# First layer of a two-layer decoder step: projections in the order gates, queries, keys, values, cached keys paced with them, convolution norm on the token axis

## The chip, the cores and the metric

The kernel runs on one core of a Trainium2 chip. The metric is the device time of one execution in microseconds; less is better. TensorE multiplies (PE in the rows, PEld is its weight load), VectorE (DVE), ScalarE (ACT) and GpSimd (POOL) do elementwise work, and SyncE (SP, SPq in the rows) issues nearly all DMAs, strictly in the order in which the program writes them. The order of the other engines' instructions is set when the program is built, and each engine then runs its own list in order.

## What is computed

Two layers, each a mixer and a squared-ReLU MLP, with norms around them, for a prompt of 1024 tokens and 8 samples of 4 tokens (1056 columns together). The change is in the mixer of the first layer:

```python
proj = xn @ w_in                       # 1024 -> 2560: q 512, k 512, v 512, a 512, g 512
s = einsum(q, k) * scale               # 4 heads, two key maps each, causal
w = softmax(map 0) - lam * softmax(map 1)
attn = rms_norm(w @ v, subln_g) * (1 - lam_init)
u = a * sigmoid(g)
c = causal_depthwise_conv(u, 31 taps) + conv_b
c = silu(layer_norm(c over its 512 channels) * ln_g + ln_b)
mixed = concat(attn, c) @ w_out
```

The samples attend to 2048 cached keys and values each, read page by page (128 tokens) through a page table, and to their own new keys and values. New keys and values of all tokens are outputs, too.

## The kernel before

Activations lie as [channel, token] in 48 slabs of [128, 1056] fp32; a tile waits until a slab is free. Products of fp32 accuracy are three matmuls of 352 columns: each operand is split into a high and a low part, and TensorE adds hi*hi, hi*lo and lo*hi (`mm3`, L195 to L197). A weight unit is a load (`wraw`), a cast on ScalarE (L188) and a subtraction on VectorE (L189).

`mixer0` (L1488) does the 20 units of the input projection one after another in the order of `seq`: `12` to `15` are a, `16` to `19` are g, `0` to `3` are q, `4` to `7` are k, `8` to `11` are v. Each unit is three blocks of 24 matmuls, one for each chunk of 352 columns (`part`), and `whole` does what follows a finished unit.

Beside this foreground run background generators. After each block the foreground calls `pump(us)`, and each generator advances by that time multiplied by its rate, which is how instructions of several strands are interleaved as they are written:

- `convs` (rate CV): 31 taps for each of four channel blocks, one `scalar_tensor_tensor` of 1024 columns each on VectorE (L977). It adds up the four blocks on GpSimd (`cn`, L996), stores each block to `cd`, waits until all projections are written (`projected`) and starts `conv_norm`, which loads the four blocks again and normalises over channels.
- `decode_k` (rate RKI during the projections, RK after): loads pairs of key pages (`load`, three pairs ahead), turns them on TensorE (`turn`, L1142, evacuated on ScalarE or, after the projections, half on VectorE at L1147), and multiplies them with the samples' queries (`strips`, L1154); then the new keys and the softmax (`dec_softmax`) for each of two groups of samples.
- `decode_v` (rate RV): 64 pairs of value pages, multiplied with the weights (L1217).
- `tokens` turns the keys and the values into token rows for the outputs; the values are also stored to `vd`, from which each head loads them in the layout that its product needs.

After the projections comes `prompt` (L1431): for four heads and eight blocks of 128 queries each, `scores` (L1324 to L1372: two score products `sp`, maximum, exponential, difference), one block later `turn` (L1386, tile `wT`), and then `values` (L1401, tile `av`). At the block number TH it starts `conv_half`, which waits for `normed` and does the convolution's half of the output projection (24 blocks of 12 matmuls, tile `y`, L1099). `finish` (L1718) turns the attention's results (`aT`, L1729) after `head_norm` (GpSimd, L1420 to L1428) of the last head; then come weight preparations, the norm of the samples' result (`subln`, whose column sum is at L1029), and the attention half of the output projection with the post norm (`posts`).

Of the kernel before, what the change touches and what calls it, by code (L numbers as in the profile page):

```python
# [16 lines left out]
P = 128  # L17
# [822 lines left out]
LEADK, LEADV, RKI, RK, RV, SMW = 3, 6, 0.45, 1.4, 1.1, 6.0  # L840
# [4 lines left out]
TH, RC, RE = 24, 1.0, 1.0  # L845
KA, SL = 1, 1.0
CV, CN, DL = 0.7, 1.0, 5.0


class Step0(Step):  # L850
# [3 lines left out]
    def consts0(self):  # L854
# [67 lines left out]
        nc.vector.tensor_scalar(self.cv[:, 5:9], self.cv[:, 5:9], -1.0, None, op0=ALU.mult)  # L922
# [58 lines left out]
    def convs(self, tiles, cd):  # L981
# [3 lines left out]
        for k in range(4):  # L985
# [51 lines left out]
    def conv_norm(self, s, cd):  # L1037

        nc = self.nc
        acc = [self.S("acc") for _ in range(4)]  # L1040
        for k in range(4):
            self.dma(acc[k], cd[k])
        yield DL
# [12 lines left out]
        yield 4.0  # L1056
        yield from self.rows_rsqrt(s, T, 512, r)
        for k in range(4):
            nc.vector.tensor_mul(acc[k], acc[k], r)
            yield 2.0  # L1060
# [4 lines left out]
        self.normed = True  # L1065

# [59 lines left out]
    def decode_k(self, qs, ks):  # L1126
# [28 lines left out]

        for i in range(LEADK):
            load(i)
# [4 lines left out]
        for i in range(64):  # L1162
# [19 lines left out]
            if pr == 7:  # L1182
                while not self.kready:
                    yield 1.0
                sc = self.PS("sc")
                strips(sc, g, slice(0, NS), lambda s, h: ks[:, 32 * h:32 * h + 32])
                nc.vector.tensor_add(SB[:, NP:T], sc[:, :NS], self.nmask[g])
                yield 0.5
                self.bg_add(self.dec_softmax(g, SA, SB), 1.0)

    def decode_v(self, vs, aS):
# [3 lines left out]
        while not self.ready:  # L1195
# [85 lines left out]
    def head_load(self, h, qd, kd, vd):  # L1281

        q, v = self.S("q"), self.S("v")
# [5 lines left out]
        vv = v[:, :1024].rearrange("p (i d) -> p i d", i=8)  # L1289
# [1096 lines left out]
```

## Time and profile before

| | us |
|---|---|
| median of 3 runs (2711.63 to 2716.34) | 2712.2 |
| the profiled execution | 2710.83 |
| its span | 2709.1 |
| TensorE busy | 2524.2 (93%) |
| VectorE busy | 1709.3 (63%) |
| ScalarE busy | 1016.9 (38%) |
| GpSimd busy | 738.3 (27%) |

The shares are means over stages with different limits; the table by stage in the rows below tells more. A busy TensorE is not one at its peak: a matmul's end is modelled, and consecutive matmuls overlap, so the time that one takes of the queue is read from the starts of the next. The granted clock is a mean over the stretch, and it has two levels, 1.2 and 2.4 GHz: 1.00 is the upper all through, 0.50 the lower.

### The profile page before, as it was taken

The numbers are of one execution on the slowest core, as the hardware profiler recorded it, in microseconds if no ns is written. First come the engines' busy times: TensorE is split into PE (matmuls) and PEld (weight loads), VectorE is DVE, ScalarE is ACT, GpSimd is POOL, SyncE is SP. The second block draws the span as 40 slices with busy tenths as digits, with TensorE's granted clock in tenths as the row PEclk, the third lists the DMA queues.
The fourth block names the chain that finished last, engine by engine and source line by source line (L and its number), as shares of the span: only waits on it lengthen the run. The fifth ranks groups of instructions, "written<-read, shape, count | busy, mean of one in ns | idle before, by whom it ended". The sixth has DMA issues, their size and how long they took to land. (4 is left out here: it accounts for less than half of the span.)

```text
span 2709.1 us, 42679 instructions
## 1 busy us (share of the span) xinstructions
PE 2524.2 (93%) x16315; PEld 2392.4 (88%) x16315; DVE 1709.3 (63%) x3036; ACT 1016.9 (38%) x2034; POOL 738.3 (27%) x1090
## 2 busy tenths in 40 slices
PE   8999979789899999999999787799879999999998
PEld 7999855559799999999999776699779999999997
DVE  6777666763868554655545999951686767455435
ACT  6133345754441222222213466642552333412103
POOL 0110001112616875343402588710510000000004
PEclk9999989999999999999999899899889999999999
DMA  5353689663032223222222433213032233433221
GB/s 187 93 170 112 202 269 318 188 222 106 14 113 63 91 82 96 61 79 82 90 78 67 168 111 111 67 35 125 22 128 95 96 116 132 174 95 110 87 80 65
DMA packets 240868, 311.41 MB, mean 115 GB/s; under 512 B 27604, under 2 KB 168162, under 8 KB 240655
## 3 DMA queue, kind: packets, MB, share of 16 engines
q1 hardware_dynamic: 240331, 308.44, 35.3%
q8 instruction: 129, 2.11, 0.3%
q14 instruction: 76, 0.62, 0.1%
q10 hardware_dynamic: 332, 0.23, 0.0%
HBM read 235.33 MB, written 73.72 MB: 114 GB/s over the span
## 5 line engine op out<-in xcount | busy, mean ns | idle before, releaser
L195 PE MATMUL mm<-hh,whi 128*128 128x352 f32 x1536 | 498.2, 326 | 0.0
L197 PE MATMUL mm<-hh,wlo 128*128 128x352 f32 x1536 | 496.6, 323 | 0.0
L196 PE MATMUL mm<-hl,whi 128*128 128x352 f32 x1536 | 496.3, 323 | 0.0
L195 PE MATMUL mm<-zh,whi 128*128 128x352 f32 x1344 | 447.3, 334 | 0.2 <-ACT zh L218 0.2
L196 PE MATMUL mm<-zl,whi 128*128 128x352 f32 x1344 | 439.8, 327 | 3.2 <-DVE zl L219 3.2
L197 PE MATMUL mm<-zh,wlo 128*128 128x352 f32 x1344 | 437.3, 326 | 0.0
L293 POOL TENSOR_TENSOR ssq<-ssq,sq 128x352 f32<-128x352 f32 x72 | 72.8, 1011 | 935.6 <-ACT sq L292 934.8
L189 DVE TENSOR_TENSOR wlo<-wraw,whi 128x1024 fp32r<-128x1024 f32 x152 | 194.7, 1284 | 168.7 <-ACT whi L188 158.6
L196 PEld LDWEIGHTS mm<-hl,whi 128*128 128x128 f32 x1536 | 289.4, 188 | 0.5 <-issue 0.2
L195 PEld LDWEIGHTS mm<-hh,whi 128*128 128x128 f32 x1536 | 289.1, 188 | 0.6 <-issue 0.2
L197 PEld LDWEIGHTS mm<-hh,wlo 128*128 128x128 f32 x1536 | 289.1, 188 | 0.0
L188 ACT CAST whi<-wraw 128x1024 fp32r<-128x1024 f32 x152 | 158.6, 1047 | 284.2 <-DMA wraw<-in_w_ffn_down 153.8
L196 PEld LDWEIGHTS mm<-zl,whi 128*128 128x128 f32 x1344 | 257.0, 191 | 7.2 <-DVE zl L219 4.0
L195 PEld LDWEIGHTS mm<-zh,whi 128*128 128x128 f32 x1344 | 256.8, 191 | 5.8 <-issue 3.0
L197 PEld LDWEIGHTS mm<-zh,wlo 128*128 128x128 f32 x1344 | 256.8, 191 | 0.1
L597 DVE TENSOR_TENSOR y<-y,mm 128x352 f32<-128x352 f32 x312 | 155.1, 517 | 76.8 <-PE mm L197 74.9
L563 ACT ACTIVATE t<-t 128x352 f32<-128x352 f32 x96 | 47.7, 498 | 318.5 <-DVE t L562 318.5
L195 PE MATMUL mm<-xh,whi 128*128 128x352 f32 x480 | 160.5, 336 | 4.2 <-DVE xr L281 4.2
L774 DVE TENSOR_TENSOR y<-y,mm 128x352 f32<-128x352 f32 x144 | 74.9, 521 | 136.5 <-PE mm L197 136.5
L977 DVE SCALAR_TENSOR_TENSOR acc<-proj,keep,acc 128x1024 f32<-128x1024 f32 x120 | 156.3, 1303 | 3.0
L196 PE MATMUL mm<-xl,whi 128*128 128x352 f32 x480 | 157.1, 328 | 0.0
L197 PE MATMUL mm<-xh,wlo 128*128 128x352 f32 x480 | 157.1, 328 | 0.0
(533 smaller groups left out, 5532.9 us busy)
## 6 DMA issues: line engine op xcount, KB each, us to landing
pg<-in_cache_k SPq DMA_DIRECT2D x128, 256.0 KB
pg<-in_cache_v SPq DMA_DIRECT2D x128, 256.0 KB
wraw<-in_w_ffn_down SPq DMA_DIRECT2D x64, 512.0 KB
wraw<-in_w_ffn_up SPq DMA_DIRECT2D x36, 512.0 KB
hr<-hid SPq DMA_DIRECT2D x32, 528.0 KB
wq<-in_w_ffn_up SPq DMA_DIRECT2D x28, 512.0 KB
hres<-res SPq DMA_DIRECT2D x24, 528.0 KB
res<-y SPq DMA_DIRECT2D x24, 528.0 KB
```

Source lines behind the costliest of these rows:

```text
L188: nc.scalar.copy(hi[:, :n], raw[:, :n])
L189: (eng or nc.vector).tensor_sub(lo[:, :n], raw[:, :n], hi[:, :n])
L195: nc.tensor.matmul(out, wh, xh, start=first, stop=False)
L196: nc.tensor.matmul(out, wh, xl, start=False, stop=False)
L197: nc.tensor.matmul(out, wl, xh, start=False, stop=last)
L293: (nc.vector if k in YV else nc.gpsimd).tensor_add(s, s, q)
L563: nc.scalar.activation(t1, t1, AF.Square)
L597: nc.vector.tensor_add(yc, yc, pt)
L774: nc.vector.tensor_add(yc, yc, pt)
L977: nc.vector.scalar_tensor_tensor(acc[:, :NP], u[:, i:i + NP], w[:, k, i:i + 1], acc[:, :NP], op0=ALU.mult, op1=ALU.add)
```

## The change

Values and keys change places in `seq`, so that the keys are known four units before the projections end. Key pages are paced at 0.85 in place of 0.45, taps at 0.85 in place of 0.7, and `conv_half` may start at block 14 in place of 24. `decode_k` no longer waits for the new keys in its line: a finished group is kept in `held`, and `fresh` adds the new keys when they are there. The last block of the convolution stays on chip, and `conv_norm` is another one: it subtracts the mean straight from PSUM, sums the squares by matmuls of one column, so that the sums lie on the token axis (one number for each token, ten columns), takes the root there on VectorE with whole numbers and three Newton steps (`root`), and brings it back with a diagonal matmul for each block. The head's values are loaded apart from its q and k (`values_load`), in the second block of each head, and the first head's load of q and k follows the first key unit. `decode_v` waits for `projected` and for the samples' values.

```diff
-LEADK, LEADV, RKI, RK, RV, SMW = 3, 6, 0.45, 1.4, 1.1, 6.0
+LEADK, LEADV, RKI, RK, RV, SMW = 3, 6, 0.85, 1.4, 1.1, 6.0
-TH, RC, RE = 24, 1.0, 1.0
+TH, RC, RE = 14, 1.0, 1.0
-CV, CN, DL = 0.7, 1.0, 5.0
+CV, CN, DL = 0.85, 1.0, 5.0
...
-            self.dma(cd[k], a)
-            a = None
+            if k < 3:
+                self.dma(cd[k], a)
+                a = None
         while not self.projected:
             yield 1.0
-        self.bg_add(self.conv_norm(s, cd), CN)
+        gen = self.conv_norm(s, a, cd)
+        next(gen)
+        self.bg_add(gen, CN)
...
-        q, r = self.S("cq"), self.S("cr")
         for c in range(NCH):
             pt = self.PS("cs")
             nc.tensor.matmul(pt[:, :CH], self.ones.bitcast(F32), s[:, chunk(c)], start=True, stop=True)
-            nc.scalar.activation(r[:, chunk(c)], pt[:, :CH], AF.Copy, scale=1.0 / 512)
-            yield 0.6
+            for k in range(4):
+                a = acc[k][:, chunk(c)]
+                nc.vector.scalar_tensor_tensor(a, pt[:, :CH], -1.0 / 512, a, op0=ALU.mult, op1=ALU.add)
+                yield 0.6
+        rows = [b for c in range(NCH) for b in blocks(c)]
...
         for k in range(4):
-            nc.vector.tensor_sub(acc[k], acc[k], r)
-            nc.scalar.activation(s if k == 0 else q, acc[k], AF.Square)
-            if k:
-                nc.vector.tensor_add(s, s, q)
-            yield 2.5
-        yield 4.0
-        yield from self.rows_rsqrt(s, T, 512, r)
-        for k in range(4):
-            nc.vector.tensor_mul(acc[k], acc[k], r)
-            yield 2.0
+            sq.append(self.S("cq"))
+            nc.scalar.activation(sq[k], acc[k], AF.Square)
+            yield 1.1
+        for i, (t, n) in enumerate(rows):
+            for k in range(4):
+                nc.tensor.matmul(pt[:n, i:i + 1], sq[k][:, t:t + n], self.ones.bitcast(F32)[:, 0:1], start=k == 0, stop=k == 3)
...
+        self.root(x, y, t_)
+        yield 3.0
+        for c in range(NCH):
+            rb = self.PS("rb")
+            for t, n in blocks(c):
+                i = rows.index((t, n))
+                dg = self.H("t")[:, :P]
+                nc.vector.tensor_scalar(dg[:n, :n], self.ident[:n, :n], y[:n, i:i + 1], None, op0=ALU.mult)
+                nc.tensor.matmul(rb[:, t - c * CH:t - c * CH + n], self.ones.bitcast(F32)[:n, :], dg[:n, :n], start=True, stop=True)
+            yield 1.0
+            for k in range(4):
+                a = acc[k][:, chunk(c)]
+                nc.vector.tensor_mul(a, a, rb[:, :CH])
+                yield 0.6
...
+    def root(self, x, y, t):
+        nc = self.nc
+        nc.vector.tensor_copy(t, x.bitcast(I32))
+        nc.vector.tensor_scalar(t, t, -0.5, 1597463007.0, op0=ALU.mult, op1=ALU.add)
+        nc.vector.tensor_copy(y.bitcast(I32), t)
+        for _ in range(3):
+            nc.vector.tensor_mul(t, y, y)
+            nc.vector.tensor_mul(t, t, x)
+            nc.vector.tensor_scalar(t, t, -0.5, 1.5, op0=ALU.mult, op1=ALU.add)
+            nc.vector.tensor_mul(y, y, t)
...
+        held = []
+        def fresh():
+            while held and self.kready:
+                g, SA, SB = held.pop(0)
+                sc = self.PS("sc")
+                strips(sc, g, slice(0, NS), lambda s, h: ks[:, 32 * h:32 * h + 32])
+                nc.vector.tensor_add(SB[:, NP:T], sc[:, :NS], self.nmask[g])
+                self.bg_add(self.dec_softmax(g, SA, SB), 1.0)
...
-        while not self.ready:
+        while not (self.ready and self.projected and self.vready):
             yield 1.0
...
+    def values_load(self, h, vd):
+        v = self.S("v")[:, :1024].rearrange("p (i d) -> p i d", i=8)
+        self.dma(v, vd[:NP, h * P:(h + 1) * P].rearrange("(i p) d -> p i d", p=P))
+        return v
...
-                    raw[h + 1] = self.head_load(h + 1, qd, kd, vd)
+                    raw[h + 1] = self.head_load(h + 1, qd, kd)
+                if i == 1:
+                    for _ in self.vgen:
+                        pass
+                    V[h] = self.values_load(h, vd)
...
-        seq = [16, 12, 17, 13, 0, 1, 2, 3, 18, 14, 19, 15, 8, 9, 10, 11, 4, 5, 6, 7]
+        seq = [16, 12, 17, 13, 0, 1, 2, 3, 18, 14, 19, 15, 4, 5, 6, 7, 8, 9, 10, 11]
...
-                    if h == 1:
-                        first.append(self.head_load(0, qd, kd, vd))
+                    if h == 0:
+                        first.append(self.head_load(0, qd, kd))
...
-                    self.bg_add(self.tokens(list(kv), T, put_v), 0.2)
+                    self.vgen = self.tokens(list(kv), T, put_v)
+                    self.bg_add(self.vgen, 1.0)
```

Three places show how the instructions move. The first is TensorE between two blocks of the projections, four units before their end: key turns `kT` (four to a row) between the last matmul of one block and what follows. Before:

```order
L197 MATMUL mm_2891<-xh_106,wlo_2518 128x352
L1142 MATMUL kT_2919<-ident,pg_2671 128x128 x4
L1142 MATMUL kT_2934<-ident,pg_2791 128x128 x4
L1142 MATMUL kT_2940<-ident,pg_2791 128x128 x4
L1482 MATMUL tok_2946<-ident,proj_2013 128x128
```

And in the changed kernel, between two blocks of its last unit:

```order
L197 MATMUL mm_3959<-xh_106,wlo_3243 128x352
L1183 MATMUL kT_3996<-ident,pg_3871 128x128 x4
L1183 MATMUL kT_4002<-ident,pg_3871 128x128 x4
L1183 MATMUL kT_4017<-ident,pg_3892 128x128 x4
L1183 MATMUL kT_4023<-ident,pg_3892 128x128 x4
L1183 MATMUL kT_4038<-ident,pg_3987 128x128 x4
L195 MATMUL mm_4045<-xh_92,whi_3579 128x352
```

The turns between blocks become more: counted over the whole list, 264 stand ahead of the first score product before, all 512 in the changed kernel.

The second is SyncE where the first head's values are read back (`v<-vd`). Before, key pages follow:

```order
L96 DMA kd<-proj_2890 128x1056
L96 DMA q_3087<-qd 128x1024
L96 DMA k_3089<-kd 64x1024 x2
L96 DMA k_3090<-kd 64x1024 x2
L96 DMA v_3088<-vd 128x8x128
L1107 TENSOR_LOAD ptab
L96 ISA
L96 DMA pg_3127<-in_cache_k 128x512
```

In the changed kernel it stands directly behind the values' token stores, ahead of the convolution's blocks and the first value pages:

```order
L96 DMA out_new_v_prompt<-tok_4321 128x512
L96 DMA vd<-tok_4321 128x512
L96 DMA out_new_v_sample<-tok_4330 32x512
L96 DMA v_4334<-vd 128x8x128
L96 DMA acc_4352<-cd 128x1056
L96 DMA acc_4353<-cd 128x1056
L96 DMA acc_4354<-cd 128x1056
L1148 TENSOR_LOAD ptab
L96 ISA
L96 DMA pg_4374<-in_cache_v 128x512
```

What the first value product needs is now written, stored and read back within the attention's first blocks.

The third is ScalarE between the last cast of the attention's result (`zh<-aT`) and the square `sq` for the samples' column sum, behind which the output product stands on TensorE. Before (from the last two weight casts on):

```order
L188 CAST whi_6955<-wraw_6952 128x1024
L188 CAST whi_6961<-wraw_6958 128x1024
L1099 COPY y_6978<-mm_6979 128x352
L1099 COPY y_6978<-mm_6993 128x352
L1099 COPY y_6978<-mm_7007 128x352
L1099 COPY y_7021<-mm_7022 128x352
L1099 COPY y_7021<-mm_7036 128x352
L1099 COPY y_7021<-mm_7050 128x352
L1099 COPY y_7064<-mm_7065 128x352
L1099 COPY y_7064<-mm_7079 128x352
L1099 COPY y_7064<-mm_7093 128x352
L1099 COPY y_7107<-mm_7108 128x352
```

In the changed kernel:

```order
L1792 ACTIVATE zh_7182<-aT_7184,gain_h 128x512
L1792 ACTIVATE zh_7182<-aT_7191,gain_h 128x512
L188 CAST whi_7201<-wraw_7198 128x1024
L188 CAST whi_7207<-wraw_7204 128x1024
L188 CAST whi_7213<-wraw_7210 128x1024
L188 CAST whi_7219<-wraw_7216 128x1024
L188 CAST whi_7225<-wraw_7222 128x1024
L188 CAST whi_7231<-wraw_7228 128x1024
L1527 ACTIVATE sq_7234<-keep_109 128x128
```

The copies of the convolution's half have gone from here to blocks of the attention: 216 of its 288 matmuls stand ahead of the last score product on TensorE, none before.

## Rows read from the trace of the kernel before

**Rows 1.** Windows: us, busy PE, PEld, DVE, ACT, POOL (instructions), clock, DMA share, GB/s

```profile
14.50:333.70 319.20, 308.02 (x2095) 291.87 (x2095) 226.04 (x290) 113.57 (x203) 28.51 (x29) 0.96 0.46 147
333.70:411.20 77.50, 59.38 (x471) 42.74 (x469) 48.45 (x116) 39.14 (x102) 2.42 (x1) 0.87 0.83 264
411.20:480.40 69.20, 63.98 (x483) 40.91 (x480) 48.12 (x115) 37.15 (x102) 7.27 (x21) 1.00 0.97 318
480.40:539.30 58.90, 46.52 (x361) 32.19 (x359) 44.47 (x118) 43.54 (x103) 7.46 (x21) 0.94 0.56 168
539.30:587.60 48.30, 38.12 (x214) 22.54 (x210) 34.69 (x91) 30.67 (x79) 8.13 (x21) 0.89 0.81 275
587.60:609.80 22.20, 20.05 (x126) 14.81 (x126) 9.61 (x21) 8.96 (x25) 0.00 (x0) 1.00 0.38 118
609.80:658.20 48.40, 46.43 (x298) 43.96 (x297) 17.41 (x25) 24.47 (x48) 8.86 (x21) 1.00 0.33 96
```

**Rows 2.** Timeline of TensorE in the projections: start, us, what, count

```profile
166.39 1.47 PE L1142 MATMUL kT<-ident,pg 128*128 128x128 f32 x12
167.62 0.41 PE L195 MATMUL mm<-xh,whi 128*128 128x352 f32 x1
...
171.57 1.47 PE L1142 MATMUL kT<-ident,pg 128*128 128x128 f32 x12
...
176.86 1.94 PE L1154 MATMUL sc<-kt,QB 128*32 128x256 f32 x32
178.72 0.43 PE L195 MATMUL mm<-xh,whi 128*128 128x352 f32 x1
```

**Rows 3.** Timeline of TensorE (in brackets its idle time), then a window

```profile
311.90 1.08 PE L1142 MATMUL kT<-ident,pg 128*128 128x128 f32 x4 [3.96 <-DMA pg<-in_cache_k]
...
312.00:319.00 7.00, 7.00 (x32) 6.98 (x33) 0.16 (x1) 0.75 (x2) 0.00 (x0) 0.63 0.36 138
```

**Rows 4.** DMA from 333.7 to 610 us: bytes, then issues with their sizes

```profile
DMA packets 37709, 68.29 MB, mean 247 GB/s; under 512 B 3728, under 2 KB 9872, under 8 KB 37680
...
pg<-in_cache_v SPq DMA_DIRECT2D x128, 256.0 KB
pg<-in_cache_k SPq DMA_DIRECT2D x58, 256.0 KB
```

**Rows 5.** Timeline of TensorE in the first head, two waits

```profile
343.35 0.45 PE L1386 MATMUL wT<-ident,p 128*128 128x128 f32 x1 [6.63 <-DVE p L1372]
...
375.90 1.94 PE L1142 MATMUL kT<-ident,pg 128*128 128x128 f32 x8 [7.45 <-DMA pg<-in_cache_k]
```

**Rows 6.** Timeline of TensorE, GpSimd, ScalarE: from attention's end to the product

```profile
607.14 2.62 PE L1401 MATMUL av<-v,wT 128*128 128x128 f32 x22
...
615.46 6.26 POOL L1428 TENSOR_SCALAR at<-at,keep 128x128 f32<-128x128 f32 x8
...
632.83 1.27 ACT L1731 ACTIVATE zh<-aT,gain_h 128x512 fp32r<-128x512 f32 x2
...
635.49 4.84 ACT L188 CAST whi<-wraw 128x1024 fp32r<-128x1024 f32 x5
...
658.16 0.38 PE L1029 MATMUL cs<-sq,ones 128*128 128x128 f32 x2
```

**Rows 7.** Timeline of TensorE: value products of two heads, and of pages

```profile
394.99 1.93 PE L1217 MATMUL O<-pg,PT 128*32 128x512 f32 x16
...
488.30 3.51 PE L1401 MATMUL av<-v,wT 128*128 128x128 f32 x30
...
551.52 5.70 PE L1401 MATMUL av<-v,wT 128*128 128x128 f32 x30
```

**Rows 8.** Groups by line, 333.7 to 610 us: count, busy us, mean ns

```profile
L977 DVE SCALAR_TENSOR_TENSOR acc<-proj,keep,acc 128x1024 f32<-128x1024 f32 x9 | 11.4, 1272 | 0.0
L1033 DVE SCALAR_TENSOR_TENSOR cn<-cs,cn 128x352 f32<-128x352 f32 x3 | 1.6, 524 | 1.0 <-ACT cn L1031 1.0
L1145 ACT COPY kt<-kT 128x512 f32<-128x512 f32 x31 | 17.8, 591 | 23.1 <-PE kT L1142 23.1
```

More of the change, by code (lines that the diff above doesn't have):

```diff
@@ L1035, in rows_rsqrt, with conv_norm @@
             yield 1.0
-    def conv_norm(self, s, cd):
+    def conv_norm(self, s, last, cd):
         nc = self.nc
-        acc = [self.S("acc") for _ in range(4)]
-        for k in range(4):
+        acc = [self.S("acc") for _ in range(3)]
+        for k in range(3):
             self.dma(acc[k], cd[k])
+        acc.append(last)
+        last = None
         yield DL
-        q, r = self.S("cq"), self.S("cr")
         for c in range(NCH):
@@ L1058, in conv_norm @@
-        for k in range(4):
-            nc.vector.tensor_mul(acc[k], acc[k], r)
-            yield 2.0
+            for k in range(4):
+                a = acc[k][:, chunk(c)]
+                nc.vector.scalar_tensor_tensor(a, pt[:, :CH], -1.0 / 512, a, op0=ALU.mult, op1=ALU.add)
+                yield 0.6
+        s = None
+        rows = [b for c in range(NCH) for b in blocks(c)]
+        pt = self.PS("vs")
+        sq = []
+        for k in range(4):
+            sq.append(self.S("cq"))
+            nc.scalar.activation(sq[k], acc[k], AF.Square)
+            yield 1.1
@@ new lines, in conv_norm @@
+        for i, (t, n) in enumerate(rows):
+            for k in range(4):
+                nc.tensor.matmul(pt[:n, i:i + 1], sq[k][:, t:t + n], self.ones.bitcast(F32)[:, 0:1], start=k == 0, stop=k == 3)
+        sq = None
+        yield 2.0
+        m = self.V(48)
+        x, y, t_ = (m[:, 16 * j:16 * j + 10] for j in range(3))
+        nc.vector.memset(m, 1.0)
+        x3, p3 = (z[:, 0:9].rearrange("p (c i) -> p c i", i=3) for z in (m, pt))
+        for n, v, q in ((P, x3[:, :, 0:2], p3[:, :, 0:2]), (96, x3[:, 0:2, 2:3], p3[:, 0:2, 2:3]), (64, m[:, 8:9], pt[:, 8:9]),
+                        (NS, m[:, 9:10], pt[:, 9:10])):
+            nc.vector.tensor_scalar(v[:n], q[:n], 1.0 / 512, 1e-5, op0=ALU.mult, op1=ALU.add)
@@ L1182, in decode_k @@
             if pr == 7:
[L1183 to L1189, printed above, removed]
+                held.append((g, SA, SB))
+            fresh()
+        while held:
+            yield 1.0
+            fresh()
     def decode_v(self, vs, aS):
@@ L1431, in prompt @@
     def prompt(self, first, qd, kd, vd, at, when, then):
-        raw, hd = {}, {0: first}
+        raw, hd, V = {}, {0: first}, {}
         blk = [(h, i) for h in range(4) for i in range(8)]
@@ L1447, in prompt @@
                 pcs[t] = []
-                yield from self.scores(i, hd[h][:2], st, hs[h], pcs[t])
+                yield from self.scores(i, hd[h], st, hs[h], pcs[t])
                 if i == 7 and h < 3:
@@ L1516, in mixer0 @@
         tiles, kv, u = [], [], []
-        self.normed = self.projected = self.kready = False
+        self.normed = self.projected = self.kready = self.vready = False
         def part(i, c, pt=None):
@@ L1606, in put_v @@
                 nc.scalar.copy(vS[:NS, :], st[:NS, :512])
+                self.vready = True
         first = []
+        self.weights, self.ready = [], False
         ahead = [self.gains(["g_mix_post", "g_ffn_pre", "g_ffn_post"]), self.consts0(), self.conv_state()]
@@ L1667, in mixer0 @@
             prep(i + 2)
+            if i == 12:
+                self.lam()
             if i == NX + 4:
@@ L1674, in mixer0 @@
         at = []
-        self.lam()
-        self.weights, self.ready = [], False
         self.projected = True
```

17 lines of the change are left out of this document (7 added, 10 removed).

## The prediction

> **What bounds the kernel now.** I read the table of busy time by stage first [rows 1]. The stages are the projections of the first layer (up to 333.7 us), four heads of prompt attention, called head 0 to head 3 (333.7, 411.2, 480.4, 539.3 and 587.6 are the ends of the projections and the last score products that open the next head), the last turns and values (to 609.8), and what stands between the last value product and the first product of the attention half (to 658.2). Nothing before 130 us and nothing after 658.2 us moves on any engine in a way that I can price, so the whole sum is about when the row at 658.16 comes: the column sum behind which the output product starts [rows 6].
>
> In the projections TensorE is the bound: 308 of 319 us busy at a mean granted clock of 0.96, with the DMA engines 46% busy [rows 1]. In the attention it is not: in the four heads it shows 59, 64, 47 and 38 us of work in 77.5, 69.2, 58.9 and 48.3, and it ran for parts of them at its lower level (means of 0.87, 1.00, 0.94, 0.89). The DMA engines are 83% and 97% busy in the first two. That stretch carries 68.29 MB, of which 58 cached key pages make 15.2 and 128 value pages 33.6 [rows 4]. So TensorE waits there for pages (7.45 us at 375.90) and for VectorE (6.63 us at 343.35) [rows 5]. From 609.8 to 658.2 it is full again: it does the convolution's half of the output projection, which had hardly begun earlier.
>
> **The change part by part.**
>
> *Cached keys.* With the pacing rate at 0.85, TensorE's order has all 512 key turns before the first score product; before, it had 264. So 248 turns and 131 rows of strips (two matmuls each in the trace, so 262) go from the attention into the projections, with 17 turns of softmax weights. Twelve turns take 1.23 us of the queue (166.39 to 167.62), or 0.1025 each; 32 strip matmuls take 1.86 (176.86 to 178.72), or 0.058 each [rows 2]. That is 25.4 + 15.2 + 1.7 = 42.3, say 42 us, and in a stage where TensorE is full nothing hides it. Their 62 evacuations, all on ScalarE there, of 0.591 us each (37 us) [rows 8] fit into a stage that it fills to 114 of 319 [rows 1].
>
> *Key pages on the DMA queue.* 15.2 MB join a stage of 147 GB/s [rows 1]; over some 245 us that is 62 GB/s more, well under the 318 that head 1 sustained [rows 1]. What can go wrong is SP, which issues in order: the loads of the first head's q and k wait for the key's own store. Before, TensorE then stood 3.96 us for a page at 311.90, and the next 7 us had a mean clock of 0.63, that is partly the lower level, worth some 2.6 us [rows 3]. This place stays (now in the first key unit, with over twice as many pages queued behind it), and the token stores come in front of pages too. I add 5 us; the ends are -3 (no such wait at all) and +15 (three waits like that of 311.90 with their slow stretches, 6.6 each, less the one there already). Projections end at 333.7 + 42 + 5 = 381.
>
> *Convolution.* CV at 0.85 ends the taps inside the projections: nine of 1.27 us, 11.4 us of VectorE [rows 8], leave the attention for a stage where VectorE has 93 us free [rows 1]. Cost nothing; without that cover 11 us.
>
> *Norm.* On VectorE it had 11 passes of 1056 columns and 6 of 352, at the taps' 1.27 and at 0.524 [rows 8] 17 us in all; now it has 24 passes of 352 columns from PSUM, like those of 0.524, 12.6 us, and some 30 tiny ones, about 19 together. ScalarE loses the copies, the root and its table loads. TensorE gets 40 products of one column (80 in the trace). No such row exists; between the strip's 0.058 and twice the turn's 0.1025 they cost 5 to 16 us, and I take the turn's own, 8 us, because its weights are as wide.
>
> *Heads.* I take each head as measured and move its work. Counts are from TensorE's order, prices from [rows 2, 7].
> Head 0: 100 turns and 128 strips go (17.7), 20 value matmuls at 0.12 (16 in 1.93) and three sums come (3.4): 77.5 - 14.3 = 63; fewer VectorE copies and a higher clock help, but the values of the layer, projected last, must pass through DRAM before TensorE's first value product, ahead of them 17 token stores, behind them three convolution loads. I take 62.
> Head 1: 124 turns, 100 strips go (18.5); 24 value matmuls, the column products and broadcasts come (13): 63.7. With the queue no longer at 97% I take 59.
> Head 2: 24 turns, 92 strips, 17 softmax turns go (9.6); 36 value matmuls (4.3) and 126 matmuls of the convolution's half (24 take 3.95, from 167.62 to 171.57, so 20.7) come: 74.3 if nothing overlaps, 62 if they fill the 12.4 us in which TensorE was idle. The norm's ScalarE passes leave this head as well: 59.
> Head 3: 52 value matmuls go (6.2), 84 of the half come (13.9): 56, or 46 if they fill its 10.2 idle us. I take 46.
> Tail: 22.2 with 16 value matmuls gone (1.9) and 2 of idle time: 18.
> Sum 244 against 276.1, ends 222 and 265. So the attention ends at 625.
>
> *To the product.* Before, 48.4 us, all covered by matmuls of the half. Now 27 of these are left behind the last value product (4.4 us), and a chain is bare: 12.0 us from the last value product to the end of the scaling on GpSimd (609.76 to 621.72), 1.7 for the last head's turns (0.4) and its two casts (1.27), then on ScalarE 5.8 for six weight casts of 0.97 that stand in front of the square for the samples' sum, and 0.7 for that square and sum: 20 us [rows 6]. TensorE is idle in it for some 10 us, and after such gaps it ran at its lower level: 30 value matmuls took 5.70 us at 551.52 against 3.51 at 488.30 [rows 7]. I add 4. So 24, ends 19 (casts early, clock held) and 33 (weights for the next stage landing late). The start of the product is 625 + 24 = 649, against 658.
>
> **The rivals.** *Attention runs at the pace of a head without key turns.* Head 3 took 48.3 us [rows 1]; if heads 1 to 3 all do, the attention is 62 + 145 + 18 = 225, and the product starts at 630: 28 us less, 2684. For it: conv matmuls fall into idle time. Against: heads 1 and 2 now hold the pages that head 3 did not.
> *The value pages bind.* By TensorE's order all value pages are used 26 blocks into the 32, 2.3 heads in. In that time they, the layer's own values out and back, q, k, convolution and output weights, some 51 MB, must pass, beginning some 13 us after the projections. At the attention's mean of 247 GB/s [rows 4] they need 206 us, then some 40 for the remaining blocks and the tail's 18: 277 us, as long as before, and the product starts at 682: 2736. At head 1's 318 GB/s [rows 1] it is 13 + 160 + 58 = 231. It decides from about 280 GB/s downwards, where the attention takes 253 and the product starts as before. For it: pages of 256 KB with few in advance. Against: 318 was reached with just such pages. A middle of 265 GB/s gives 263, 2722.
> *Nothing on balance:* what goes out of the attention comes back in the projections and in the bare chain (waits of 10 to 15 us instead of 5): within 5 us of 2712.
> *The clock falls in the projections.* If turns did not hold the clock up, the 248 that come would run at the lower level, 25 us more than forecast, 2728. Against it: head 1, with 124 turns and not one of the wide matmuls, had a mean clock of 1.00 [rows 1]. The Trainium skill has this rule (TensorE: Matmul & The Clock Gate, Part 4: PE-mode transpose): a transpose doesn't count as activity that raises the clock. By it this rival would be likely; the trace disagrees in head 1.
>
> **How the numbers follow.** The profiled execution took 2710.8 us against a median of 2712.2, so 1.4 more is added: 658.2 to 649 is 9 us less, 2703. Forecast (2692 to 2712) 0.42; the pace of head 3, 0.20; value pages, 0.20; nothing on balance, 0.15; clock, 0.03. 0.2% is 5.4 us, about what a measurement of this kernel can tell from no change. Two parts in three of the forecast's range lie beyond that; with the first rival and a little of the case that balances the chance of faster is 0.50. Slower is value pages, clock and a little of that same case, 0.26; the rest, 0.24, is the same. The range reaches through the first rival into the middle of the second: 2678 to 2727. The forecast's own is 2692 to 2712.
>
> **What would show it.** The first prompt score product at 376 to 390 us, no kernel time lost to pages in the projections beyond two waits of about 5 us; DMA in the attention 50 to 53 MB instead of 68; score products of the four heads 55 to 65 us apart and the last near 47; TensorE idle in a chain like that from 609.8 to 621.7 and ScalarE's casts ending just ahead of the samples' sum. It is wrong if the first score comes after 392, if the attention takes more than 253 us, or if head 2 grows by the full 20 us of the half.

## The result, and the profile of the changed kernel

The changed kernel takes 2742.8 us (median of four runs, 2734.7 to 2745.5) against 2711.9 for the kernel before, measured in the same session: a ratio of 1.0108, 95% interval 1.0082 to 1.0135. I had said 2703 and a range of 2678 to 2727. It is slower, by 31 us, and outside the range. The profiled run took 2745.5 us, with a span of 2743.4; it is the longest of the four, and its span is 34.3 us over that of the kernel before.

Nearly all of the loss stands ahead of the output product. This timeline of TensorE shows the first score product and the samples' column sum behind which the product starts (before, they stood at 333.7 and 658.16 [rows 1, 6]):

```profile
408.29 0.39 PE L1378 MATMUL sp<-kh__411_2996,qp 128*128 128x256 f32 x1
...
689.40 0.80 PE L1031 MATMUL cs<-sq,ones 128*128 128x128 f32 x2 [6.65 <-ACT sq L1527]
```

The column sum comes at 689.40 instead of 658.16, 31.2 us later, of the 34.3 by which the two profiles differ. The stages by windows (same columns as [rows 1]: us; busy PE, PEld, DVE, ACT, POOL with instructions; granted clock; DMA share; GB/s): end of the projections from 130 us on, head 0, head 1, head 2, head 3 with the tail, and the chain to the product.

```profile
130.00:408.30 278.30, 256.89 (x1949) 223.73 (x1947) 151.61 (x147) 106.28 (x193) 17.57 (x15) 0.95 0.55 168
408.30:491.07 82.77, 65.56 (x414) 42.41 (x411) 44.67 (x132) 37.80 (x96) 0.00 (x0) 0.79 0.91 310
491.07:550.37 59.30, 47.00 (x294) 30.27 (x293) 39.84 (x113) 34.30 (x88) 8.14 (x21) 0.86 0.71 246
550.37:613.63 63.26, 60.65 (x381) 42.32 (x377) 42.15 (x106) 36.35 (x100) 7.55 (x21) 1.00 0.67 201
613.63:670.00 56.37, 54.18 (x369) 48.08 (x369) 29.41 (x96) 27.20 (x91) 7.82 (x21) 1.00 0.16 48
670.00:689.40 19.40, 10.21 (x60) 8.03 (x58) 13.57 (x19) 14.99 (x26) 9.10 (x21) 0.77 0.68 230
```

Against the forecast: projections end at 408 (381 forecast), head 0 takes 82.8 (62), heads 1 and 2 59.3 and 63.3 (59 each), head 3 with the tail 56.4 (64), the chain 19.4 (24). Two of the signs of being wrong that I had named came: the first score after 392 us, and an attention of more than 253. Two terms carry the whole error: the projections, 27 too short, and head 0, 21 too short; the other three together were 8 too long. Head 0 gave up its 100 key turns and got longer. Its idle TensorE time hardly moved: 77.50 less 59.38 is 18.1 us before [rows 1], 82.77 less 65.56 is 17.2 now. But it isn't the same idle time. TensorE's waits in head 0 (waiter, releaser, us in total, times, longest), before and then in the changed kernel:

```profile
PE wT L1386 <- DVE p L1372: 10.4, 2, 6.6
PE kT L1142 <- DMA pg<-in_cache_k: 7.7, 2, 7.5
```

```profile
PE O L1267 <- DMA pg<-in_cache_v: 9.6, 3, 5.3
PE wT L1440 <- DVE p L1426: 7.6, 1, 7.6
```

The waits for key pages went with the turns, and waits for value pages came in their place.

The groups of TensorE up to 408.3 us (count; busy us, mean ns; idle time ahead and its releasers) show the moved turns and what they wait for; in the same view of the kernel before, the turns were 264 with 9.2 us of waits and the strips 256 with 0.1.

```profile
L1183 PE MATMUL kT<-ident,pg 128*128 128x128 f32 x512 | 68.7, 285 | 11.1 <-DMA pg<-in_cache_k 10.2 <-ACT tok L1542 0.7 <-ACT proj L1614 0.2
L1195 PE MATMUL sc<-kt,QB 128*32 128x256 f32 x486 | 42.0, 399 | 8.2 <-ACT kt L1186 8.0
```

### The profile page after: what moved, and what is told of

Same layout as the page of the kernel before. It is cut to its first block, busy times and chain, and to the rows that moved or that the text cites. A ratio compares the mean times of both kernels' runs of the same rounds, so it can differ in the third digit from the quotient of the medians.

```text
span 2743.4 us, 42892 instructions
## 1 busy us (share of the span) xinstructions
PE 2549.3 (93%) x16409; PEld 2407.2 (88%) x16409; DVE 1696.1 (62%) x3041; ACT 1022.9 (37%) x2051; POOL 744.8 (27%) x1090
## 5 line engine op out<-in xcount | busy, mean ns | idle before, releaser
L597 DVE TENSOR_TENSOR y<-y,mm 128x352 f32<-128x352 f32 x312 | 155.8, 518 | 78.4 <-PE mm L197 76.6
```

The costliest lines, as they stand in the source:

```text
L597: nc.vector.tensor_add(yc, yc, pt)
```

## The experiments

"Projections end", "head 0", "attention" (from the start of the first score product to that of the last value product) and "product" (start of that column sum) are read from each kernel's timeline of TensorE:

| kernel | time, us | ratio to before, 95% | projections end | head 0 | attention | product |
|---|---|---|---|---|---|---|
| before | 2711 | | 333.7 | 77.5 | 275.8 | 658.2 |
| changed | 2742.8 | 1.0082 to 1.0135 | 408.3 | 82.8 | 261.4 | 689.4 |
| u_pace | 2706.1 | 0.9967 to 0.9997 | 329.0 | 88.4 | 297.1 | 646.8 |
| u_order | 2708.9 | 0.9974 to 1.0000 | 330.5 | 84.5 | 296.5 | 648.5 |
| u_norm | 2732.6 | 1.0050 to 1.0110 | 397.5 | 72.1 | 245.6 | 665.8 |
| b_pace | 2716.0 | 0.9998 to 1.0024 | 327.0 | 80.8 | 282.7 | 658.3 |
| x_noturn | 2681.3 | 0.9871 to 0.9909 | 356.1 | 81.4 | 258.6 | 634.3 |
| x_nopage | 2722.4 | 1.0025 to 1.0054 | 386.1 | 82.2 | 260.9 | 666.6 |
| pace60 | 2724.6 | 1.0030 to 1.0069 | 360.1 | 96.3 | 285.2 | 665.0 |
| pace25 | 2746.8 | 1.0100 to 1.0151 | 341.5 | 83.8 | 320.4 | 695.5 |
| lead4 | 2755.0 | 1.0146 to 1.0180 | 419.3 | 81.0 | 259.1 | 698.3 |
| stores_pool | 2735.5 | 1.0067 to 1.0103 | 398.5 | 82.9 | 262.9 | 681.3 |
| norm10 | 2742.1 | 1.0094 to 1.0131 | 403.7 | 75.6 | 258.2 | 684.3 |
| u_pace_norm | 2706.5 | 0.9974 to 1.0001 | 324.7 | 85.9 | 300.0 | 649.0 |
| x_novalue | 2722.6 | 1.0027 to 1.0060 | 399.2 | 81.2 | 245.6 | 664.6 |
| half_only | 2706.5 | 0.9963 to 0.9985 | 331.3 | 78.4 | 290.5 | 646.1 |
| half_stores | 2693.9 | 0.9912 to 0.9955 | 326.0 | 72.4 | 286.6 | 636.9 |
| p45_stores_norm10 | 2710.5 | 0.9985 to 1.0006 | 327.2 | 80.0 | 299.3 | 654.1 |
| soft_late | 2747.2 | 1.0101 to 1.0152 | 401.8 | 82.1 | 267.6 | 689.2 |
| pages_first | 2737.8 | 1.0079 to 1.0131 | 399.9 | 83.1 | 258.3 | 678.1 |

One caution: five kernels here have the changed kernel's work up to the first score product (u_norm, norm10, x_novalue, soft_late and pages_first). In their profiles, the sister profiles below, that product comes between 397.5 and 403.7. So 408.3 is a long draw by 5 to 10 us, and a stage's end in one profile is good to about that.

### Pacing, order, norm

**u_pace.** In the changed kernel:

```
-LEADK, LEADV, RKI, RK, RV, SMW = 3, 6, 0.85, 1.4, 1.1, 6.0
+LEADK, LEADV, RKI, RK, RV, SMW = 3, 6, 0.45, 1.4, 1.1, 6.0
```

> The changed kernel with one edit undone: the pacing rate of the cached keys in the projections back at 0.45, so that about half of the key turns fall into the attention again. Theory 'turns in a full stage' (the 248 turns and their strips cost the projections their full price and stalls, 74.6 us, and the attention gives only 14 back): projections end at about 350 us instead of 408, the attention grows by less than 40, and the time falls by 15 to 40 us, to 2700 to 2728. Theory 'values last' (head 0 loses its 17 us of idle TensorE time and as much at the lower clock because the layer's own values and the value pages start only when all projections are done): that loss stays and the key turns come on top of it; 2735 or more.

36.7 us come off, a little more than the whole loss. Projections end 79 us earlier (58 was expected) and the attention is 36 longer. "Turns in a full stage" holds, "values last" as the cause of the loss falls.

**u_order** is the kernel before with the new norm, RKI = 0.85, TH = 14 and CV = 0.85. **b_pace** is the kernel before with RKI = 0.85 alone.

> The changed kernel with the order undone: queries, values, keys, with what belongs to it (value pages from the end of the projections, the values loaded with the head's keys); pacing 0.85, the new norm, the earlier half and the faster taps stay. Theory 'values last': head 0 shrinks from 82.8 to 60 to 68 us and the time falls by 12 to 25 us, to 2718 to 2730. Theory 'turns in a full stage': the projections still end near 400 to 408, the time stays within 8 us of 2743.

> The kernel before with one edit alone: the pacing rate at 0.85. Theory 'turns in a full stage': projections end 55 to 75 us later than 333.7, the attention shrinks by less than that, since its first heads are paced by value pages and VectorE too; 2720 to 2745, slower than before. Theory 'values last' (the pacing itself is harmless): 2690 to 2715, not slower than before.

I expected b_pace to be slower if turns are dear; it is the same as before, within 0.2%, and u_order is too, outside the ranges of both theories. The reason is in the code and not in a price. In the old order the keys are projected last, and after the first half of the pages the key step waits for them:

```
-                while not self.kready:
-                    yield 1.0
```

By TensorE's order both kernels still have 264 turns ahead of the first score product, as before. The rate alone moves none; only with the new order and its list of held groups does 0.85 pull all 512 forward. So these two runs don't set pacing against order, as I had meant; they show that the loss needs both. The order without the rate is u_pace, and it loses nothing. Which part of the order does it, the changed places in `seq` or the list of held groups, was not tried apart.

**u_norm** puts the norm of before back into the changed kernel; **u_pace_norm** does the same with RKI = 0.45; **norm10** keeps the new norm but sums the squares on GpSimd first, 10 products for 40:

```
+            if k:
+                nc.gpsimd.tensor_add(sq[0], sq[0], sq[k])
```

> The changed kernel with the convolution's norm of before (root over all columns on ScalarE, no one-column products). Theory 'the norm's products': TensorE is relieved of 82 one-column products (11.9 us at 473 to 485, a stretch with a mean granted clock of 0.61) and 20 broadcasts (3.0 us), and the time falls by 8 to 15 us, to 2728 to 2735. Rival, 'head 0 is bound by pages anyway': the products fill time in which TensorE would wait for value pages; within 5 us of 2743, or a few us slower, since VectorE and ScalarE get the passes back.

> The changed kernel with two edits undone: pacing rate 0.45, and the norm of before. With pace 0.85 the norm of before took 10 us off (2733 against 2743), no more than the intervals allow for. Theory 'the norm's products' (TensorE's 11.9 us for one-column products and 3.0 for broadcasts are on the path of the first two heads): 8 to 15 us less than with the pace alone, 2691 to 2698. Rival 'they fill idle time' (with key turns back, the first heads wait for pages, and the norm hides there): 2702 to 2710.

> The changed kernel with the four squares of the norm summed on GpSimd first (three passes), so that TensorE does 10 one-column products instead of 40. Theory 'the norm's products' (82 matmul records, 11.9 us, on the path of head 0): 6 to 10 us less, 2733 to 2737. Rival 'hidden behind the value pages': within 4 us of 2743.

The three don't agree on a gain: 10 us less (its interval overlaps a little with that of the changed kernel), none, none. What u_norm and norm10 do show is head 0. With the norm of before it took 72.1 us instead of 82.8; the window has

```profile
397.50:469.70 72.20, 56.99 (x347) 28.76 (x344) 38.77 (x101) 36.52 (x93) 0.00 (x0) 0.88 0.92 313
```

so TensorE's busy time is 8.6 us less and the clock higher. norm10, whose products fall into head 1, shortens head 0 by 7 us, but the later stages and the chain keep most of that. So at the rate of 0.85 the one-column products lengthened head 0 by 7 to 11 us, and of the whole time the norm is worth between nothing and 10 us; at the rate of 0.45 it is worth nothing. It isn't the main cause.

### What the moved turns pay in the projections

**x_noturn** (`if i >= 32:` one turn of eight, no strips) and **x_nopage** (`raw[i] = raw.get(31) or raw[i - 1]` for those pages) leave out one half of the price each. With the turns and strips x_noturn also leaves out their evacuations on ScalarE.

> The changed kernel, leaving out work: of the second 32 cached key pages only one of eight key turns is done, and none of their strips and evacuations (copies of the same size from another tile stand in for the scores); every page is still loaded. Undoing the pace took 80 us off the projections and gave the attention 36 more. Theory 'work' (TensorE's own price of the moved turns and strips is most of the 80): projections end at 345 to 362 instead of 408. Theory 'queue' (about half of the 80 is waits for pages behind other transfers on SP, and the lower clock after them): those stay, and projections end at 370 to 385.

> The changed kernel, leaving out the loads of the second 32 cached key pages: TensorE turns one page that is kept, again and again, so all its work stays. Theory 'work': projections end at 395 to 405. Theory 'queue': the waits for pages (10.2 us) and what follows from them go, projections end at 370 to 388.

Each theory hit its range in one of the two. Without the work the projections end 52 us earlier, without the transfers 22 us; together that is 74, what the stage had grown. Against the 400 of the sister profiles it is 44 and 14. The work, ScalarE's part in it included, is the larger part, but the pages cost a good deal more than the 5 us that I had given them. How they do it shows in TensorE's waits from 240 us to the end of the projections (waiter, releaser, us in total, times, longest), first of the changed kernel, then of x_nopage:

```profile
PE sc L1195 <- ACT kt L1186: 8.0, 2, 4.6
PE kT L1183 <- DMA pg<-in_cache_k: 6.1, 2, 5.2
PE mm L195 <- ACT tok L1542: 1.5, 1, 1.5
```

```profile
PE kT L1185 <- DMA pg<-in_cache_k: 5.1, 1, 5.1
PE pT L1319 <- DVE SA L1309: 1.3, 1, 1.3
PE sc L1197 <- ACT kt L1188: 0.2, 1, 0.2
```

It is not mainly the wait for a page. The strips waited 8.0 us for ScalarE's evacuations, and that goes without the pages. The two waits of the strips, and what ScalarE did just ahead of each (timelines of ScalarE and TensorE):

```profile
295.46 1.04 ACT L188 CAST whi<-wraw 128x1024 fp32r<-128x1024 f32 x1 [5.23 <-DMA wraw<-in_w_in_even]
297.80 1.07 ACT L1186 COPY kt<-kT 128x512 f32<-128x512 f32 x2 [0.94 <-DVE wlo L189]
298.92 3.62 PE L1195 MATMUL sc<-kt,QB 128*32 128x256 f32 x26 [3.47 <-ACT kt L1186]
...
334.87 1.07 ACT L1186 COPY kt<-kT 128x512 f32<-128x512 f32 x2 [1.45 <-DMA out_new_k_prompt<-tok]
335.99 1.06 PE L1195 MATMUL sc<-kt,QB 128*32 128x256 f32 x2 [4.56 <-ACT kt L1186]
```

ScalarE works in order, and so a weight cast that came late, and later the copies and stores of key tokens, held the key evacuations behind them. In all ScalarE stood still for a weight (17.3 us in three waits from 200 to 345 us) and for the stores of key tokens, and SP, which issues weights, token stores and pages in one order, stood, as I read its waits, for page buffers that a turn had to free and for token copies that it had to store (same stretch):

```profile
ACT whi L188 <- DMA wraw<-in_w_in_even: 17.3, 3, 6.7
ACT tok L1542 <- DMA out_new_k_prompt<-tok: 5.9, 5, 2.2
SPq L96 <- PE kT L1183: 15.8, 8, 4.6
SPq L96 <- ACT tok L1542: 13.5, 8, 2.8
```

Without the second half of the pages the waits for weights fall to 7.4 us. A late weight alone isn't the cost, though: in u_pace ScalarE waits 27.2 us for weights from 200 us on, and TensorE, with 280 turns in the stage instead of 512, loses 0.3 us from 240 us on. The clock follows the waits: 0.94 from 250 us to the end of the projections in the changed kernel, 0.98 without the pages.

**stores_pool** tests that chain: the stores of tokens and of convolution rows are issued by GpSimd instead of SP (`nc.gpsimd.dma_start(dst, st[:n, :512])`).

> The changed kernel with the stores of tokens (keys and values for the caches) and of the convolution's rows issued on GpSimd's queue instead of SP's, so that pages and weights no longer stand behind them. TensorE's order is the same. Theory 'SP's order': the wait of 5.2 us at 254.57 and the waits on token copies and key evacuations from 319 to 338 go (some 12 us with their stretches at the lower clock), and in head 0 the layer's values and the first value page come earlier; projections end at 385 to 398, time 2720 to 2733. Rival 'the pages' own bytes': the projections end at 400 or later, time within 5 us of 2743.

The projections end at 398.5, a shade outside the range of "SP's order" and no earlier than in the sister profiles, and the time falls by 7 us, with intervals that overlap. Page waits from 240 us on are gone, but one of 6.4 us for ScalarE stands there instead, and ScalarE still waits 18.5 us for weights (20.7 in the changed kernel from 240 us on). So the stores' part of the chain isn't shown in this kernel, and the 7 us stay open; what x_nopage takes off belongs to the pages.

**lead4** loads four pages ahead, **pace60** and **pace25** set RKI to 0.6 and 0.25.

> The changed kernel with four key pages loaded ahead in place of three. Theory 'queue': one page more covers some 3 us of each of the waits of 5.2 and 4.6 us; projections end 5 to 12 us earlier, time 2730 to 2738. Theory 'work': within 4 us of the changed kernel's 2743.

> The changed kernel with the pacing rate at 0.6: by TensorE's order 368 key turns stand ahead of the first score product, against 280 with 0.45 and 512 with 0.85. If the cost is even in the turns (theory 'work': each turn with its strips costs the projections 0.34 us and gives the attention 0.15 back), a third of the way from 2706 to 2743: 2716 to 2722. If the first ones are free and the price comes with the crowding at the end, where the token stores, the first head's loads and the last pages meet (theory 'queue'): 2700 to 2711.

> The changed kernel with the pacing rate at 0.25: 168 key turns ahead of the first score product, against 280 with 0.45 (2706 us), 368 with 0.6 (2725) and 512 with 0.85 (2743). Theory 'even price' (each turn with its strips costs the projections 0.34 us and gives the attention 0.15 back, wherever one stands): 112 turns fewer take 15 to 25 us off, 2680 to 2692. Rival 'the attention is full by then' (its first two heads have the DMA engines over 90% busy, and 3 us of pages for every page that moves there come on top): 2704 to 2725.

lead4 was a miss of both theories, 12 us slower. pace60 lies a little above the range of "work" and far from that of "queue". pace25 is outside both of its ranges. In lead4 and pace25 TensorE waits once for a token copy, 22.1 and 31.1 us. Timeline of ScalarE in pace25:

```profile
252.33 0.58 ACT L1186 COPY kt<-kT 128x512 f32<-128x512 f32 x1 [2.62 <-DVE wlo L189]
284.33 0.58 ACT L1542 COPY tok<-tok 128x512 f32<-128x512 f32 x1 [31.42 <-DVE acc L976]
```

The copy of the key tokens waits for the convolution's taps on VectorE, whose results it doesn't read. All large tiles come from one pool of buffers, and I take it that the token tile got one that the taps still read; that wasn't tested apart. With this wait of 31.1 taken off, pace25 would be near 2716 by my estimate, in the rival's range; that fewer than 280 turns ahead bring nothing more is likely, then, but not shown. pace60 has 88 turns more than u_pace for 18 us, 0.21 us each, and the changed kernel 144 more than pace60 for another 18, 0.13 each. By the times alone the price doesn't wait for the crowding at the end. But pace60 has two single waits of TensorE for VectorE, 6.6 us ahead of the first score product and 9.9 behind it, and so what a single turn costs isn't shown.

### Why head 0 didn't shrink

**soft_late** (a yield of 30 ahead of the second softmax) and **pages_first** (value pages issued ahead of `while not self.vready`):

> The changed kernel with the softmax of the second half of the cached keys put off by some blocks, so that its two passes on ScalarE and three on VectorE no longer stand in front of the first block's weights (TensorE waits 7.58 us at 426.48, on VectorE). Theory 'softmax at the opening': head 0 loses 7 to 12 us of its 82.8, time 2731 to 2736. Rival 'value pages': the wait moves to the first value page, which is on its way until 433; head 0 within 4 us, time within 4 of 2743.

> The changed kernel with the first six value pages issued as soon as the projections end, between the stores of the layer's own values instead of behind them. Theory 'value pages': TensorE's waits for value pages in head 0 (3.91 at 433.13, 5.31 at 455.39) shrink and head 0 loses 6 to 12 us, time 2731 to 2737. Rival 'softmax at the opening' or 'DMA's own pace' (the six pages only take the place of later ones): within 4 us of 2743.

The first says nothing on its theory: the softmax's passes stood where they had stood, 11 us behind the first score product, and the wait of 7.6 us with them. What the edit put off, from 53 us behind that product on, were the turns of the softmax's result and the value products that need them; the later heads are others (head 1 takes 51.9 us, head 3 with the tail 67.2), and the time is that of the changed kernel within the intervals. The second moved the waits (11.7 us for value pages and 4.3 for the weights, where there were 9.6 and 7.6) and left the time, 2737.8, within the interval of the changed kernel, between the ranges of its theories.

**x_novalue:**

> The changed kernel, leaving out the loads of all but the first six value pages; TensorE multiplies a page that is kept in place of the others, so its work stays. The attention of the changed kernel took 261 us (heads 82.8, 59.3, 63.3, the rest 56.4). Theory 'value pages': head 0 loses its page waits (9.6 us) and its lower clock (mean 0.79) and takes 65 to 72, the attention 235 to 248. Rival 'chain of the softmaxes' (the 7.6 us at 426 on VectorE and the waits for weights in head 1 stay, and so do the gaps that lower the clock): head 0 at 75 or more, attention 250 or more.

Half a hit for each. The attention falls by 16 us, so the value pages do bind. Head 0 stays at 81.2 for another reason than before:

```profile
399.16:480.40 81.24, 70.73 (x457) 41.31 (x454) 45.25 (x131) 36.92 (x92) 0.00 (x0) 0.85 0.49 164
```

TensorE's idle time in it falls from 17.2 to 10.5 us (the wait for value pages from 9.6 to 2.9), but with the pages at hand 114 page products are done in it instead of 72, and these are missing in head 2, which takes 52.6 us for 63.3. So the page waits of head 0 count, and what they are worth shows in a later head. What holds head 0, timeline of TensorE in the changed kernel:

```profile
426.48 0.66 PE L1440 MATMUL wT<-ident,p 128*128 128x128 f32 x2 [7.58 <-DVE p L1426]
...
433.13 6.22 PE L1267 MATMUL O<-pg,PT 128*32 128x512 f32 x18 [3.91 <-DMA pg<-in_cache_v]
...
455.39 3.42 PE L1267 MATMUL O<-pg,PT 128*32 128x512 f32 x10 [5.31 <-DMA pg<-in_cache_v]
...
473.07 11.49 PE L1066 MATMUL vs<-ones,cq 128*128 128x1 f32 x76
```

With all key turns done, the second half's softmax falls due at the opening of head 0 and its passes stand on VectorE ahead of the first weights: 7.6 us. The first value page is issued only when the layer's own values are out: 3.9, and 5.3 again. Between such gaps TensorE ran at its lower level (mean clock 0.79 against 0.87 before), and the norm's products, 80 in the trace and some 11.9 us, fell into head 0 (the 82 of the expectations counts two twice). u_norm gives them 10.7 us of the head, norm10 7.2; of the waits, only those for pages were taken off, in x_novalue. What the softmax at the opening is worth was not taken apart.

### What of the change pays

**half_only** is the kernel before with TH = 14 and CV = 0.85, nothing else; **half_stores** adds the stores on GpSimd's queue; **p45_stores_norm10** is the changed kernel with 0.45, the stores and the ten products.

> The kernel before with two numbers changed: the convolution's half of the output projection starts ten blocks earlier, and the taps are paced at 0.85. As the prediction had it (its matmuls fill time in which TensorE is idle in heads 2 and 3, and the chain behind the last value product is 24 us instead of 48): 2690 to 2700. Rival 'no idle time to fill' (the half's 35 us of matmuls lengthen the attention nearly by themselves, as 296.5 against 276.1 suggests where the new norm came with them): 2703 to 2713.

> The kernel before with the earlier half and the taps at 0.85 (2706 us), and with the stores of tokens and convolution rows on GpSimd's queue. With the changed kernel that move took some 7 us off. Theory 'SP's order': the wait for a page at the end of the projections shrinks and pages of the first head come earlier; 2697 to 2703. Rival: the projections have one such wait only; within 4 us of 2706.

> A candidate: the changed kernel with the pacing rate at 0.45, the stores on GpSimd's queue and the norm with 10 products. If what the two cost with 0.85 is on the path here as well: 2706 less 3 to 8 for the products and less 3 to 10 for the stores, 2690 to 2700. If the first heads wait for the DMA engines whatever TensorE does: 2702 to 2710.

half_only lands in the rival's range, faster than before by 0.15 to 0.37%: the chain behind the last value product falls from 48.4 to 24.1 us, and the attention takes 14.7 back. It has both the earlier half and the faster taps; they were not run apart. half_stores beats both kernels, 0.9933 (0.9912 to 0.9955), 17 us. Its windows (projections from 130 us on, then head 0), under those of half_only:

```profile
130.00:331.30 201.30, 194.64 (x1405) 182.55 (x1406) 142.33 (x133) 66.52 (x117) 18.58 (x15) 0.96 0.50 164
331.30:409.70 78.40, 59.94 (x471) 41.21 (x469) 45.96 (x114) 43.71 (x109) 0.00 (x0) 0.91 0.84 273
```

```profile
130.00:325.90 195.90, 190.24 (x1404) 178.57 (x1405) 141.72 (x133) 66.64 (x117) 27.30 (x33) 0.98 0.53 168
325.90:398.30 72.40, 57.56 (x463) 40.91 (x461) 45.16 (x113) 43.53 (x105) 5.07 (x9) 0.91 0.87 295
```

The projections end 5.3 us earlier, with TensorE 4.4 us less busy at a clock of 0.98 for 0.96, and head 0 loses 6.0 us. Of half_only's waits in it the one for a token copy is gone, and ScalarE's wait ahead of that copy, for an earlier token store to land, falls from 9.2 to 1.9; the waits for pages grew, to 9.4. In half_only:

```profile
PE kT L1142 <- DMA pg<-in_cache_k: 6.7, 2, 3.8
PE wT L1386 <- ACT tok L1484: 5.7, 1, 5.7
ACT tok L1484 <- DMA out_new_k_prompt<-tok: 9.2, 1, 9.2
```

The Trainium skill (DMA: Bandwidth & Descriptors, Issuing engines are not separate DMA queues) says that issuing from several engines saves only the sequencer's time, usually small beside the transfer. Here 12.6 us lie between the two medians, 0.4% by their ratios. I read it so that a store stands in SP's order until its producer is done and all behind it stands too; the wait of 5.7 us bears that out for less than half, the rest is not taken apart. The ten products with a rate of 0.45 added nothing to that: p45_stores_norm10 missed its range and is the same as before.

## Why the prediction was wrong, step by step

**What bounds the kernel:** right. 31.2 of the 34.3 us between the profiles lay where I had put the sum, and TensorE was nearly full in the projections: 257 of 278 us from 130 us on.

**Count of moved turns:** right, 512 ahead of the first score product, 264 before. I took it from TensorE's order, and it holds for the whole change only; b_pace shows that the rate alone would have moved none.

**"42 us, and in a stage where TensorE is full nothing hides it":** mis-sized. I price each family by the time from one start to the next, less the named waits. Up to the first score product the turns take 62.1 us instead of 31.1, 31.0 more (25.4 forecast), the strips 40.5 instead of 16.8, 23.7 more (15.2), the projections' own matmuls 3.3 more at the same count. The forecast priced turns and strips at full clock and in long unbroken rows; here they stand in short groups, partly at the lower level. With the smaller families that is 61; against the 400 of the sister profiles the whole stage is some 66 longer instead of 74.6, so a part of these sizes is the draw.

**"I add 5 us":** the step that failed by its nature. The idle time before the first score product grew from 15.2 to 28.9 us. I looked for waits for pages and allowed three; these grew by 1 us, from 9.2 to 10.2, and the new ones, 11 us, were for ScalarE, which waited for weights and token stores. In all 74.6 us for a term of 47, and the upper end, 42 + 15, didn't reach it either. The ends don't follow from their own prices, besides: three waits of 6.6 us less the one that is there are 13 and not 15, and no wait at all is 6.6 less and not 3.

**Head 0, "I take 62":** failed. The step "100 turns and 128 strips go: 77.5 - 14.3" let the head shrink by the work taken out. But the idle time of 18 us stayed: the 7.7 us for key pages went, 9.6 for value pages came, and the softmax's wait changed little (10.4 and 7.6). The clock went down, 0.87 to 0.79, where I had said it would rise. And the norm's products came in here and not in head 1, which is 7 to 11 of the 21 us by norm10 and u_norm. All in all the turns left the attention for less than they cost: u_pace against the changed kernel says 36 us back for 79 paid; by my rows it was to be 46 for 47.

**The norm:** the products took 11.9 us, within the 5 to 16 forecast; what they cost the whole time the runs leave open between 0 and 10 us.

**Heads 1 to 3 and the chain:** right in sum, 179 us for 182 and 19.4 for 24, and the half's matmuls did fill idle time: 2.6 us are left of the 12.4 in head 2. The half put forward costs less than the chain loses, and half_only shows it by itself, but smaller than I had it: 0.26%, 5 us, where I expected 12 to 22.

**Rivals:** "value pages bind" named a true limit (x_novalue: 16 us of the attention) and the wrong stage. Its 2736 lies nearest to the result by luck: it had the attention at 277 us, and it took 261. "The clock falls in the projections" came true in small, 0.94 from 250 us on, but after waits, not by the turns: from 350 to 408 us TensorE did 120 key turns, 17 turns of softmax weights and 120 strip matmuls among 199 wide ones, at a clock of 1.00, as the window shows. Neither this window nor head 1 shows what turns alone would do:

```profile
350.00:408.30 58.30, 58.30 (x465) 50.87 (x457) 3.84 (x5) 22.49 (x44) 1.46 (x1) 1.00 0.40 118
```

## What to carry to other kernels

Work that was moved here from a stage that waits into a stage that is nearly full was paid above its own price where it arrived, while the stage that it left shrank by about half of that (79 and 36 us by u_pace, 71 and 36 with the sister profiles' end). So price both ends, and ask for each wait of the old stage whether the moved work made it and what takes its place when it goes. Where engines and one issuing queue work in order, count what stands behind a new transfer on that queue, which engine waits for it, and what work stands close behind that engine: the pages cost 1 us as pages, and 14 to 22 with what came of them. And try the parts of a change apart: here a small part was the gain, and the loss came only where two parts met.

## What the runs showed of the hardware that I had not expected

TensorE's granted clock fell during the one-column products, although the engine shows no idle time in them. Windows of 2 us in the changed kernel, with all but four of the products from 473.1 to 484.6:

```profile
472.00:474.00 2.00, 2.00 (x12) 1.15 (x11) 1.93 (x9) 2.00 (x5) 0.00 (x0) 1.00 0.74 251
474.00:476.00 2.00, 2.00 (x20) 2.00 (x19) 0.81 (x2) 2.00 (x7) 0.00 (x0) 0.89 0.98 311
476.00:478.00 2.00, 2.00 (x11) 2.00 (x11) 1.88 (x5) 1.98 (x3) 0.00 (x0) 0.50 0.95 336
```

TensorE is busy 2.00 of 2.00 us and the granted clock is 0.50, that is its lower level, 1.2 GHz, until 488, and 1.00 again from 490, after softmax turns and value products. x_novalue has the same fall within its products (0.73 from 468 to 470, 0.50 from 470 on) with a DMA share of 0.00. So a full busy row doesn't say that the engine is at its upper level; the clock column has to be read with it.
